# Two down tiles in block form, and four out-projection tiles summed onto the residual in PSUM

## The chip, the cores and the metric

The kernel runs on one core of a Trainium2 chip. The metric is the time of one execution on the device, in microseconds (us). A core has engines with queues of their own, each in order: TensorE (PE: matmuls, and PEld: the loads of their weights), VectorE (DVE), ScalarE (ACT), GpSimd (POOL) and SyncE (SP), which here only issues DMAs. Matmuls read SBUF and write PSUM, eight banks of 128 x 512 fp32; VectorE and ScalarE read and write both. Semaphores join the queues.

## The reference, cut to what matters

One layer of a hybrid encoder, for 512 tokens of a new stream and 64 of a running one, 576 columns in all. State-space heads and latent-attention heads give `y_ssd` and `o`; then:

```python
x = x + jnp.concatenate([y_ssd, o], axis=-1) @ p['w_out']
hf = rmsnorm(x, p['norm_ffn'])
x = x + (jax.nn.silu(hf @ p['w_gate']) * (hf @ p['w_up'])) @ p['w_down']
...
y_prompt = rmsnorm(xp, norm_final)
```

`D_MODEL` is 1024, so `x` has 8 tiles of 128 channels; `D_FF` is 2816, 22 tiles of 128. All data are fp32.

## The kernel before

All activations lie transposed: 128 channels on the partitions, 576 tokens along the row, worked on as two halves of 288 (`TH`). An fp32 product is made of three fast ones: each operand is split into a high part (a rounding cast, by ScalarE) and a low part (the rest, a subtraction by VectorE), and the matmuls are high x high, high x low, low x high. `split_weights` (lines 113, 114) does this for every 128 x 1024 piece of weights. So each weight costs ScalarE and VectorE time as well.

**Out-projection** (`out_tile`, line 728; `product_halves`, line 441). For each tile `t` of `x`, the sum over the four attention tiles, and for some tiles over the four state-space tiles too (those of the others were added earlier, the "F" steps of the order string), goes into a bank "hm", one for each half: 12 or 24 matmuls. Its `evac` then adds the bank to the residual `x2[t]` on VectorE (line 740):

```python
        def evac(ps, cols):
            dve.tensor_tensor(x2[t][:, cols], ps, x2[t][:, cols], ALU.add)
```

The tiles come in the order O0 O1 O2 O3 O5 O4 O6 O7, with the sums of squares (Q) and the operands of the next stage (`x_operands`, lines 797 to 805: scalings and casts by ScalarE, subtractions by VectorE) between them.

**Gate and up** (`gu_steps`; `block_product`, line 871). Gate and up of one 128-channel tile `f` and the two token halves form a 2 x 2 block product, made with seven products in place of eight (the Winograd form). Sums of weights (`block_weights`, lines 827 to 830) and of operands stand for the eighth. A tile is 7 x 4 x 3 = 168 matmuls, gathered in three banks x, y, z by steps m1, m6, m7, m2, m5, m4, m3. Between the steps ScalarE or VectorE takes results out of a bank to which the next step adds on. Each tile needs seven pieces of split weights in the ten buffers of `w2pool`, and four raw ones from the eight of `wpool`.

**Down**. The 22 tiles fall into parts 0-3, 4-7, 8-11, 12-15, 16-17 and 18-21. The first four parts use the same block form (`pair`, line 980; `down_steps`, lines 1004 to 1052; `down_blocks`): two pairs of tiles `f` against two tiles of `x` at a time, 7 x 2 x 3 matmuls, the first tile's results added to `x2[t]` by VectorE, those of the second gathered by ScalarE into SBUF and added by accumulating DMAs from GpSimd's queue (line 1022). They are placed among the products of the next part's first two tiles. Tiles 16 and 17 use the plain form (`down`, line 1081; matmuls of line 1077): for each of the eight `x` tiles a weight DMA, a split of 128 x 256, two groups of six matmuls and two additions by VectorE (line 1088). Tiles 18 to 21 make the end of the kernel together with the last norm; nothing of that changes.

**Order.** The program's own order is only a start. At the end `issue_in_order` reads the lists `ISSUE`, one for each engine, and ties each instruction to the one ahead of it. So each engine's order is written out, as numbers of instructions in program order. Buffers of the pools `tpool` (7 temporaries), `wpool` (8), `cpool` (5), `w2pool` (10) and the PSUM banks "hm" (2), "sc" (3), "pp" (3) rotate.

Of the kernel before, what the change touches and what calls it, by code (L numbers as in the profile page):

```python
# [37 lines left out]
BLOCKS = tuple(range(0, LAST - 1, 4))  # L38

# [16 lines left out]
def hybrid_layer_kernel(ctx: ExitStack, tc: tile.TileContext, a, o):  # L56
# [15 lines left out]
    cpool = ctx.enter_context(tc.tile_pool(name="cpool", bufs=5))  # L72
    a_, apool = open_pool("apool", bufs=4)
# [4 lines left out]
    def slot(pl, tag, name, **kw):  # L78
        return pl.tile([P, 2, T], F32, tag=tag, name=name, **kw)

    def tmp(name, w=T):
        return tpool.tile([P, UPW], F32, tag="t", name=name)[:, :w]
# [23 lines left out]
    def wslot(wp, name, dt=F32):  # L106
        return wp.tile([P, 1024], dt, tag="w", name=name)
# [330 lines left out]
    def bank(tag, name):  # L438
        return (psq if tag == "sc" else psh).tile([P, 512], F32, tag=tag, name=name, bufs={"sc": 3, "pp": 3, "hm": 2}[tag])

    def product_halves(terms, n, name, evac, hfs=(0, 1)):

        for hf in hfs:
            ps = bank("hm", f"{name}_{hf}")
            cols = slice(hf * n, (hf + 1) * n)
            for k, ((whi, wlo), (xhi, xlo)) in enumerate(terms):
                for i, (w, x) in enumerate(((whi, xhi), (whi, xlo), (wlo, xhi))):
                    pe.matmul(  # L448
                        ps[:, :n], w, x[:, cols], start=k == 0 and i == 0, stop=k == len(terms) - 1 and i == 2,
                    )  # L450
            evac(ps[:, :n], cols)
# [276 lines left out]
    def out_tile(hfs, t):  # L728
# [13 lines left out]
        product_halves(terms, TH, f"ps_o{hfs[-1]}_{t}", evac)  # L742
# [37 lines left out]
    w2pool = ctx.enter_context(tc.tile_pool(name="w2pool", bufs=10, reuse_waits="tile"))  # L780
    xop = ctx.enter_context(tc.tile_pool(name="xop", bufs=1, reuse_waits="tile"))
# [36 lines left out]
    def block_weights(src1, src2, name, blocks):  # L818
# [4 lines left out]
        shaped = lambda z: z if len(src1.shape) == 2 else z.rearrange("p (t c) -> p t c", t=2)  # L823
# [18 lines left out]
    held, blocks, fz2 = {}, [], []  # L842
# [74 lines left out]
    def finish(f, g, u):  # L917
        act.activation(g, g, AF.Silu)
        dve.tensor_tensor(u, u, g, ALU.mult)
# [53 lines left out]
    def paired(f, u):  # L973
# [3 lines left out]
        if k == 3 or f == BLOCKS[0] + 1:  # L977
# [26 lines left out]
    def down_steps(fs, w, h, p):  # L1004

        t = 4 * h + 2 * p
        qs = blocks[(fs[0] - BLOCKS[0]) // 2 :][:2]
        x, y, z = fbank("hm", f"ps_dx{fs[0]}_{t}"), fbank("sc", f"ps_dy{fs[0]}_{t}"), fbank("pp", f"ps_dz{fs[0]}_{t}")
        B, C = (tmp(f"d{i}{fs[0]}_{t}") for i in "bc")

        def sums(ps, i, onto=False):
            n, xi = PRODUCTS[i - 1]
            for k, q in enumerate(qs):
                whi, wlo = (z[:, 2 * p + k] for z in w[n])
                o = q[xi]
                for j, (l, r) in enumerate(((whi, o[:, 0]), (whi, o[:, 1]), (wlo, o[:, 0]))):
                    pe.matmul(  # L1017
                        ps, l, r, start=not onto and k == 0 and j == 0, stop=onto or (k == 1 and j == 2), skip_group_check=onto,
                    )

        def add_to(t, v):
            pool.dma_start(x2[t], v, accum_op=ALU.add)  # L1022
# [5 lines left out]
        def m6():  # L1028
            sums(x, 6, True)
            act.copy(B[:, :TH], x)  # L1030

        def m7():
            sums(z, 7)
            act.copy(C[:, TH:], z)
# [5 lines left out]
        def m5():  # L1040
            sums(x, 5, True)
            act.copy(B[:, TH:], x)  # L1042
            add_to(t + 1, B)

        def m4():
            sums(z, 4, True)
            act.copy(C[:, :TH], z)
# [8 lines left out]
    def down_blocks(fs, h, late):  # L1056
        w = down_weights(fs[0], h)
        if fs[0] == 0 and h == 0:
            Ri = tmp("Ri")
            dve.scalar_tensor_tensor(Ri, ss3, P / (D * EPS), R2, ALU.mult, ALU.mult)  # L1060
            for t in range(KT):
                dve.tensor_tensor(x2[t], x2[t], Ri, ALU.mult)
        for p in range(2):
            first, rest, middle = down_steps(fs, w, h, p)
# [4 lines left out]

    def down_terms(fs, t):  # L1070
        w = weights(a["w_down"][t][:, fs[0] * P : (fs[-1] + 1) * P], len(fs) * P, f"d{fs[0]}_{t}")
        return [(wk(w, k), prod[f]) for k, f in enumerate(fs)]
# [7 lines left out]

    def down(fs):

        for t in range(KT):
            terms = down_terms(fs, t)
            for hf, cols in enumerate(HC):
                ps = fbank(("hm", "sc", "pp")[(2 * t + hf) % 3], f"ps_d{fs[0]}_{t}")
                down_half(ps, terms, cols)
                dve.tensor_tensor(x2[t][:, cols], ps, x2[t][:, cols], ALU.add)
# [6 lines left out]
    for part in PARTS:  # L1095
        for f in part:
# [5 lines left out]
            if len(prev) == 4 and f in part[:2]:  # L1102
                late = down_blocks(prev, f - part[0], late)
                if f == part[1]:
                    if len(part) == 4:
                        late += (lambda f=f: pair(f),)
                    else:
                        late += tuple(lambda f=f: single(f, held.pop(f)) for f in part)
# [166 lines left out]

ISSUE = {
# [13 lines left out]
1190-1192 1227 1193-1198 1291-1297 1199-1201 1228 1202-1204 1286-1288 1207-1223 1318-1319 1224-1226 1298-1317  # L1290
1330-1333 1342-1343 1348-1355 1344-1347 1320-1329 1334-1341 1356-1392 1404-1405 1393-1401 1406 1402 1407-1409 1403
1410-1418 1428 1419-1427 1429-1430 1572 1431-1434 1440-1442 1435-1436 1443-1445 1437-1439 1446-1461 1464 1462
# [267 lines left out]
```

## Time and profile before

| | us |
|---|---|
| three runs shown | 645.3, 646.35, 1577.34 |
| median of them | 646.35 |
| profiled execution, its own time | 645.34 |
| its span, first to last instruction | 643.4 |
| PE busy | 631.6 |
| VectorE busy | 544.8 |
| ScalarE busy | 381.1 |

The 1577.34 is a single run far off the other two; the profiled execution agrees with the lower ones. In the profile's views, "idle before" is the time for which an engine stood still ahead of a group of instructions, and the arrow names what ended it. Busy times of pipelined matmuls overlap, so the number of matmuls that start in a stretch tells more than the share that is busy. Names of tiles are the program's with the numbers left out: `x<-ps_o,x` is an addition of a bank of the out-projection to the residual.

### The profile page before, as it was taken

How to read it: one execution, taken by the hardware profiler on the slowest of the kernel's cores; microseconds unless marked ns; L12 is line 12 of the kernel's file. 1: busy time of each engine (PE TensorE's matmuls, PEld its weight loads, DVE VectorE, ACT ScalarE, POOL GpSimd, SP SyncE). 2: the span in 40 equal slices, each digit the busy share in tenths (PEclk: the TensorE clock that was granted, in tenths of full speed). 3: DMA queues.
4: the chain of work that ended last, by engine and by line, in shares of the span. 5: the costliest groups of instructions: out<-in, count | busy, mean ns of one | idle time of the engine just before them, and what ended most of it. 6: DMA issues, size and time to landing. Idle time of an engine off the chain costs nothing.

```text
span 643.4 us, 11975 instructions
## 1 busy us (share of the span) xinstructions
PE 631.6 (98%) x4651; PEld 600.3 (93%) x4651; DVE 544.8 (85%) x974; ACT 381.1 (59%) x733; POOL 70.4 (11%) x111
## 2 busy tenths in 40 slices
PE   9999999999999999999999999999999999999995
PEld 9799999886797899899999999999999999999994
DVE  6999986899766699999998997989689886697664
ACT  7645425879766476765557465655664655354464
POOL 1422131101000000000012002100211020100022
PEclk9999999999999999999999999999999999999999
DMA  9521184314221232142286428552646243734004
GB/s 320 193 73 56 51 206 137 112 40 135 107 76 33 100 98 73 60 132 66 66 204 152 120 78 193 121 151 66 157 143 168 74 115 67 169 127 132 1 1 147
DMA packets 31656, 72.66 MB, mean 113 GB/s; under 512 B 3802, under 2 KB 11496, under 8 KB 31344
## 3 DMA queue, kind: packets, MB, share of 16 engines
q1 hardware_dynamic: 25456, 60.77, 29.4%
q0 software_dynamic: 5424, 10.57, 9.2%
q8 instruction: 36, 0.59, 0.4%
q10 hardware_dynamic: 720, 0.57, 0.3%
q14 instruction: 20, 0.16, 0.1%
HBM read 58.03 MB, written 3.30 MB: 95 GB/s over the span
## 4 chain that ended last, share of the span: by engine, by line
PE 83%; DVE 10%; ACT 3%; issue 2%; DMA 1%; POOL 0%; POOLq 0%; DVEq 0%; ACTq 0%
PE ps_x L871 20%; PE ps_z L871 10%; PE ps_dx L1017 8%; PE ps_in L129 8%; PE ps_o L448 6%; PE ps_y L871 5%; PE ps_dz L1017 4%; PE ps_z L448 4%; PE ps_first L129 2%; PE ps_d L1077 2%; PE ps_dy L1017 2%; PE ps_l L1077 2%; PE sc L662 2%; PE pv L709 1%; PE ptp L684 1%
## 5 line engine op out<-in xcount | busy, mean ns | idle before, releaser
L871 PE MATMUL ps_x<-xop,wh_gu_S 128*128 128x288 f32 x504 | 119.2, 297 | 0.0
L871 PEld LDWEIGHTS ps_x<-xop,wh_gu_S 128*128 128x128 f32 x504 | 85.2, 188 | 1.0 <-ACT ps_y L942 0.3
L871 PE MATMUL ps_x<-xop,wl_gu_S 128*128 128x288 f32 x252 | 73.5, 295 | 0.0
L113 ACT CAST wh_gu_S<-gu 128x1024 fp32r<-128x1024 f32 x44 | 46.4, 1054 | 23.0 <-PE ps_x L871 12.0
L114 DVE TENSOR_TENSOR wl_gu_S<-gu,wh_gu_S 128x1024 fp32r<-128x1024 f32 x44 | 53.4, 1219 | 4.8 <-ACT wh_gu_S L113 4.6
L871 PE MATMUL ps_z<-xop,gu_a 128*128 128x288 f32 x252 | 52.3, 295 | 0.0
L1022 POOL DMA_DIRECT2D x<-db x16 | 14.9, 991 | 304.7 <-ACT db L1042 162.1
L871 PEld LDWEIGHTS ps_x<-xop,wl_gu_S 128*128 128x128 f32 x252 | 47.2, 188 | 0.0
L129 PE MATMUL ps_in<-xs,wh_in 128*128 128x288 f32 x256 | 45.4, 298 | 0.0
L871 PE MATMUL ps_y<-xop,wh_gu_A 128*128 128x288 f32 x168 | 43.0, 297 | 0.3 <-ACT ps_y L942 0.3
L871 PE MATMUL ps_z<-xop,wh_gu_S 128*128 128x288 f32 x168 | 41.2, 296 | 0.5 <-DVE g L954 0.5
L871 PE MATMUL ps_x<-xop,wh_gu_A 128*128 128x288 f32 x168 | 41.2, 296 | 0.1
L871 PEld LDWEIGHTS ps_z<-xop,gu_a 128*128 128x128 f32 x252 | 40.1, 188 | 0.1
L129 PEld LDWEIGHTS ps_in<-xs,wh_in 128*128 128x128 f32 x256 | 37.7, 189 | 0.2
L114 DVE TENSOR_TENSOR wl_gu_A<-gu,wh_gu_A 128x1024 fp32r<-128x1024 f32 x22 | 26.8, 1219 | 4.2 <-ACT wh_gu_A L113 3.6
L871 PEld LDWEIGHTS ps_y<-xop,wh_gu_A 128*128 128x128 f32 x168 | 29.4, 188 | 0.7 <-ACT ps_y L942 0.6
L871 PEld LDWEIGHTS ps_z<-xop,wh_gu_S 128*128 128x128 f32 x168 | 28.8, 188 | 0.9 <-issue 0.7
L871 PEld LDWEIGHTS ps_x<-xop,wh_gu_A 128*128 128x128 f32 x168 | 28.9, 188 | 0.6 <-ACT wh_gu_A L113 0.3
L448 PE MATMUL ps_o<-cat_y,wh_out 128*128 128x288 f32 x128 | 28.5, 310 | 0.0
L448 PE MATMUL ps_o<-cat_o,wh_out 128*128 128x288 f32 x128 | 27.9, 298 | 0.0
L129 PE MATMUL ps_in<-xs,wl_in 128*128 128x288 f32 x128 | 27.5, 296 | 0.0
L113 ACT CAST wh_gu_A<-gu 128x1024 fp32r<-128x1024 f32 x22 | 23.1, 1051 | 6.5 <-PE ps_x L871 4.0
(557 smaller groups left out, 1973.2 us busy)
## 6 DMA issues: line engine op xcount, KB each, us to landing
gu<-in_w_gu SPq DMA_DIRECT2D x44, 512.0 KB, 4.1
db<-in_w_down SPq DMA_DIRECT2D x16, 512.0 KB, 3.8
x<-db POOLq DMA_DIRECT2D x16, 288.0 KB, 4.8
x<-dc POOLq DMA_DIRECT2D x16, 288.0 KB, 4.2
wr_in<-in_w_in SPq DMA_DIRECT2D x8, 512.0 KB, 6.1
wr_out<-in_w_out SPq DMA_DIRECT2D x8, 512.0 KB, 3.3
cumb<-cumD SPq DMA_DIRECT2D x5, 512.0 KB, 4.3
x<-in_xT SPq DMA_DIRECT2D x2, 1152.0 KB, 5.7
```

What stands on the lines that cost most here:

```text
L113: act.copy(hi, raw)
L114: dve.tensor_tensor(lo, raw, hi.bitcast(F32), ALU.subtract)
L129: pe.matmul(ps[:m, hf, :n], w, x[:, hf * n : (hf + 1) * n], start=start and k == 0 and i == 0, stop=stop and k == last and i == 2,)
L448: pe.matmul(ps[:, :n], w, x[:, cols], start=k == 0 and i == 0, stop=k == len(terms) - 1 and i == 2,)
L662: pe.matmul(s[:, :nk], qs[:, j, q0 : q0 + P], ks[:, j, :nk], start=True, stop=True)
L684: pe.transpose(pp[:, k : k + P], prs[p, i][:, j, b * P : b * P + P], ident)
L709: pe.matmul(pv[64 * j : 64 * j + 64, b * P :], V[b][:, h * HD : (h + 1) * HD], pts[p, b, j], start=b == 0, stop=True, skip_group_check=b > 0,)
L871: pe.matmul(ps, p, q, start=not onto and first and kp == kps[0] and j == 0, stop=onto or (last and kp == kps[-1] and j == 2), skip_group_c ...
L1017: pe.matmul(ps, l, r, start=not onto and k == 0 and j == 0, stop=onto or (k == 1 and j == 2), skip_group_check=onto,)
L1022: pool.dma_start(x2[t], v, accum_op=ALU.add)
L1077: pe.matmul(ps, w, x[:, cols], start=first and k == 0 and i == 0, stop=last and k == len(terms) - 1 and i == 2,)
```

## The change

1. **Out-projection, tiles 4 to 7** (`SEEDED`). ScalarE copies the residual half into the bank, all matmuls of the half add onto it, and ScalarE copies the sum back into `x2[t]`. VectorE's addition goes. The "F" steps keep the old form.
2. **Down tiles 16 and 17** in block form. One pair of `f` tiles, so that a product has 3 matmuls in place of 6; one set of block weights for all eight `x` tiles, used while tiles 18 and 19 run; the second `x` tile's results are added by VectorE from the bank, not by DMA.
3. **Fixed slots.** Each buffer of the four pools and each PSUM bank is taken by number from strings in `PLACES`, with as many buffers as before.
4. **New orders** for PE, VectorE, ScalarE and SP; GpSimd's is the same. PE has 12 instructions fewer (4392), VectorE 6 more (980), ScalarE 18 more (720), SP 6 fewer. PE's order is unchanged up to its 1278th instruction, VectorE's up to its 353rd, ScalarE's up to its 267th, SP's up to its 78th.

```diff
+SEEDED = (4, 5, 6, 7)
...
+    kept = {id(tpool): "t", id(wpool): "w", id(cpool): "c"}
+    counts = {}
+
+    def placed(pl, shape, dt, tag, name, bufs=None):
+
+        key = kept.get(id(pl), tag)
+        n = counts[key] = counts.get(key, -1) + 1
+        return pl.tile(shape, dt, tag=f"{key}{PLACES[key][n]}", name=name, bufs=1)
...
     def bank(tag, name):
-        return (psq if tag == "sc" else psh).tile([P, 512], F32, tag=tag, name=name, bufs={"sc": 3, "pp": 3, "hm": 2}[tag])
+        return placed(psq if tag == "sc" else psh, [P, 512], F32, tag, name)
...
-    def product_halves(terms, n, name, evac, hfs=(0, 1)):
+    def product_halves(terms, n, name, evac, hfs=(0, 1), base=None):
...
+            onto = base is not None
+            if onto:
+                act.copy(ps[:, :n], base[:, cols])
             for k, ((whi, wlo), (xhi, xlo)) in enumerate(terms):
                 for i, (w, x) in enumerate(((whi, xhi), (whi, xlo), (wlo, xhi))):
                     pe.matmul(
-                        ps[:, :n], w, x[:, cols], start=k == 0 and i == 0, stop=k == len(terms) - 1 and i == 2,
+                        ps[:, :n], w, x[:, cols], start=not onto and k == 0 and i == 0,
+                        stop=onto or (k == len(terms) - 1 and i == 2), skip_group_check=onto,
                     )
...
-        product_halves(terms, TH, f"ps_o{hfs[-1]}_{t}", evac)
+        if 1 in hfs and t in SEEDED:
+            product_halves(terms, TH, f"ps_o{hfs[-1]}_{t}", lambda ps, cols: act.copy(x2[t][:, cols], ps), base=x2[t])
+        else:
+            product_halves(terms, TH, f"ps_o{hfs[-1]}_{t}", evac)
...
     def down_weights(f, h):
-        src = a["w_down"][4 * h : 4 * h + 4, :, f * P : f * P + 512].rearrange("(t i) k c -> i k t c", i=2)
+        ts, n = (slice(4 * h, 4 * h + 4), 4) if h is not None else (slice(0, KT), 2)
+        src = a["w_down"][ts, :, f * P : (f + n) * P].rearrange("(t i) k c -> i k t c", i=2)
...
-        if f < BLOCKS[-1]:
+        if f < LAST:
             return paired(f, u)
-        if f < LAST:
-            held[f] = u
-            return
-        single(f, u)
-
-    def single(f, u):
         s = slot(cpool, "c", f"pr{f}")
...
-    def down_steps(fs, w, h, p):
+    def down_steps(fs, w, t, b, by_dma=True):
...
+        def out(v, cols, ps):
+            if by_dma:
+                act.copy(v[:, cols], ps)
+            else:
+                y = x2[t + 1][:, cols]
+                dve.tensor_tensor(y, ps, y, ALU.add)
+
         def add_to(t, v):
-            pool.dma_start(x2[t], v, accum_op=ALU.add)
+            if by_dma:
+                pool.dma_start(x2[t], v, accum_op=ALU.add)
...
+        if len(fs) == 4:
+            w = down_weights(fs[0], h)
+        elif h == 0:
+            wpair[0] = w = down_weights(fs[0], None)
+        else:
+            w = wpair[0]
...
-    def down(fs):
-
-        for t in range(KT):
-            terms = down_terms(fs, t)
-            for hf, cols in enumerate(HC):
-                ps = fbank(("hm", "sc", "pp")[(2 * t + hf) % 3], f"ps_d{fs[0]}_{t}")
-                down_half(ps, terms, cols)
-                dve.tensor_tensor(x2[t][:, cols], ps, x2[t][:, cols], ALU.add)
...
-            if len(prev) == 4 and f in part[:2]:
+            if prev and f in part[:2]:
                 late = down_blocks(prev, f - part[0], late)
...
-            elif prev and f == part[0]:
-                for step in late:
-                    step()
-                late = ()
-                down(prev)
...
+PLACES = {
...
+    "v": "".join("""
+0987654321908751432968751043964387926510437926843759120647358910647235069184735062913547809613524709618354709612354780
+912356470912834509761234508971234506971283406975123064897123056497128306497512306489797129730581267430589164732
```

The string "v" gives the slots of `w2pool` in program order. Near its end stand, seven each (one piece for A22, then high and low of A11/A12, of S1/S2 and of S3/S4): gate/up tile 18 `8306497`, the pair's down weights `5123064`, gate/up tile 19 `8979712`, tile 20 `9730581`, tile 21 `2674305`, and eight pieces for the end.

More of the change, by code (lines that the diff above doesn't have):

```diff
@@ L106, in wslot @@
     def wslot(wp, name, dt=F32):
+        if id(wp) in kept:
+            return placed(wp, [P, 1024], dt, "w", name)
         return wp.tile([P, 1024], dt, tag="w", name=name)
@@ L976, in paired @@
         k = (f - BLOCKS[0]) % 4
-        if k == 3 or f == BLOCKS[0] + 1:
+        if k == 3 or f == 1:
             pair(f)
@@ L1041, in m5 @@
             sums(x, 5, True)
-            act.copy(B[:, TH:], x)
+            out(B, HC[1], x)
             add_to(t + 1, B)
@@ L1046, in m4 @@
             sums(z, 4, True)
-            act.copy(C[:, :TH], z)
+            out(C, HC[0], z)
             add_to(t + 1, C)
```

360 lines of the change are left out of this document (198 added, 162 removed).

## The prediction

> **What bounds the kernel now.** I read the page's head first, then the busy times by stretches of 20 us, then what the weight loads of TensorE waited for.
>
> ```profile
> span 643.4 us, 11975 instructions
> ## 1 busy us (share of the span) xinstructions
> PE 631.6 (98%) x4651; PEld 600.3 (93%) x4651; DVE 544.8 (85%) x974; ACT 381.1 (59%) x733; POOL 70.4 (11%) x111
> ```
>
> TensorE (PE) is busy nearly all the time, so a change can win only matmuls that no longer exist, or the small holes that are left. The stretches show where the holes are (columns: stretch, length, then busy time and instruction count of PE, weight loads, VectorE, ScalarE, GpSimd, then the granted clock).
>
> ```profile
> 220.00:240.00 20.00, 20.00 (x150) 19.63 (x149) 19.53 (x33) 12.70 (x18) 0.00 (x0) 1.00 0.41 139
> 240.00:260.00 20.00, 19.50 (x141) 18.53 (x140) 20.00 (x41) 13.75 (x24) 0.00 (x0) 1.00 0.32 107
> 260.00:280.00 20.00, 19.86 (x140) 18.62 (x139) 20.00 (x35) 14.56 (x24) 0.00 (x0) 1.00 0.17 58
> 280.00:300.00 20.00, 19.66 (x148) 19.38 (x147) 19.98 (x34) 11.25 (x18) 0.00 (x0) 1.00 0.35 107
> 300.00:320.00 20.00, 19.79 (x149) 19.49 (x148) 19.97 (x34) 11.53 (x20) 0.00 (x0) 1.00 0.17 53
> ...
> 340.00:360.00 20.00, 20.00 (x153) 20.00 (x152) 18.12 (x30) 12.88 (x22) 3.44 (x4) 1.00 0.67 165
> ```
>
> In an undisturbed stretch 153 matmuls of 288 columns start in 20 us: one every 20/153 = 0.131 us. That pace, not the length of one matmul, prices a matmul that goes. From 220 to 320 us only 728 start where 5 x 153 = 765 would fit: 37 x 0.131 = 4.8 us of pace are lost there, at most (a few matmuls in it have other shapes). In the same 100 us VectorE (DVE) is busy 99.5 us. It holds the last out-projection tiles, the operands of gate and up, and the first weight splits.
>
> ```profile
> PEld ps_p L871 <- DVE xop L805: 0.8, 2, 0.4
> PEld ps_p L871 <- ACT xop L804: 0.7, 2, 0.4
> PEld ps_y L871 <- ACT ps_y L942: 0.6, 1, 0.6
> PEld ps_o L448 <- DVE x L740: 0.5, 2, 0.3
> PEld ps_dx L1017 <- ACT ps_dy L1026: 0.5, 1, 0.5
> PEld ps_x L871 <- ACT wh_gu_A L113: 0.3, 1, 0.3
> PEld ps_x L871 <- ACT ps_y L942: 0.3, 1, 0.3
> ```
>
> These are all waits of the weight loads between 220 and 320 us: 3.7 us. Two of them name VectorE; the ScalarE (ACT) ones are operands and weights whose inputs VectorE makes (line 804 casts what lines 798 to 801 subtract). So this stretch is bound by VectorE, the rest by TensorE's pace.
>
> **Out-projection tiles 4 to 7.** Eight additions on VectorE go (two halves, four tiles; line 740). In their place ScalarE copies the residual into the bank ahead of the matmuls and the sum out behind them.
>
> ```profile
> L740 DVE TENSOR_TENSOR x<-ps_o,x 128x288 f32<-128x288 f32 x30 | 13.5, 453 | 7.0 <-PE ps_o L448 6.8
> ```
>
> ```profile
> L1034 ACT COPY dc<-ps_dz 128x288 f32<-128x288 f32 x16 | 6.5, 403 | 6.3 <-PE ps_dz L1017 5.8 <-ACT db L1042 0.4
> ...
> L1026 ACT COPY ps_dy<-ps_dx 128x288 f32<-128x288 f32 x16 | 6.1, 387 | 5.3 <-PE ps_dx L1017 5.3
> ...
> L996 ACT CAST fz<-u 128x288 fp32r<-128x288 f32 x8 | 3.5, 433 | 0.8 <-DVE u L919 0.8
> ```
>
> VectorE loses 8 x 0.453 = 3.6 us in its full stretch. A copy out is 0.403 (line 1034, PSUM to SBUF). A copy from SBUF into PSUM has no row; it lies between 0.387 (PSUM to PSUM) and 0.433 (SBUF to SBUF, with a cast), and I take 0.39, since the destination is the same. ScalarE gains 8 x 0.79 = 6.3 us between about 230 and 260 us, where it is idle 40 - 12.70 - 13.75 = 13.6 us: it fits on average.
>
> The new wait is TensorE's: the first matmul into a bank now follows copy out and copy in, 0.79 us, where it followed an addition of 0.45. Two banks ("hm") alternate, and the order written out in the change puts 8 to 11 other matmuls between the last one of a bank and the first of its next owner, 1.05 to 1.44 us: covered by 0.26 us at the tightest, hand-over included. Behind one pair of copies ScalarE's order has a 128x576 cast and a 128x1024 cast ahead of the next pair; there I expect a hole of some tenths. If the cover were gone at all eight, it would cost 8 x 0.79 = 6.3 us.
>
> What the 3.6 us are worth lies between 0 (ScalarE becomes the late engine, its casts of line 804 stand between the copies) and 4.8 us (every lost slot of the stretch returns). Adding VectorE's durations along both written orders, I find the queue ahead of the sums of tiles 1 and 2 (lines 954, 966) shorter by 3 to 5 us, which leans to the upper part. The stretch is not bound by VectorE at every moment; I take **3.0 us**. What is late next is ScalarE.
>
> **Down tiles 16, 17.**
>
> ```profile
> L1077 PEld LDWEIGHTS ps_d<-pr,wh_d x64: 187/188/189, 552.8 to 571.1; 128*128 128x128 f32 x64
> L1077 PE MATMUL ps_d<-pr,wh_d x64: 288/295/313, 553.0 to 571.2; 128*128 128x288 f32 x64
> L1077 PEld LDWEIGHTS ps_d<-pr,wl_d x32: 187/188/193, 554.0 to 572.9; 128*128 128x128 f32 x32
> L1077 PE MATMUL ps_d<-pr,wl_d x32: 290/295/310, 554.2 to 573.0; 128*128 128x288 f32 x32
> ```
>
> (Columns: shortest, median and longest in ns, then first and last start.) These 96 matmuls go. The block form has 4 pairs of output tiles x 7 products x 3 = 84. Twelve fewer at 0.131 us are **1.6 us**; the stretches in which they lie run at full pace (below), so this comes off the end. The Trainium skill (Perfetto Trace Analysis, Identifying the Most-Contended Engine) says that pipelined matmuls make matmul time a bad measure and that the busy share of weight loads is the good one; by it the twelve would be an estimated 12 x 0.188 = 2.3 us, with the 188 ns above. The loads are 93% busy where matmuls start without a hole, so the pace decides here.
>
> The other engines pay:
>
> ```profile
> L114 DVE TENSOR_TENSOR wl_db_S<-db,wh_db_S 128x1024 fp32r<-128x1024 f32 x16 | 19.4, 1220 | 1.6 <-ACT wh_db_S L113 1.5
> ...
> L1088 DVE TENSOR_TENSOR x<-ps_d,x 128x288 f32<-128x288 f32 x16 | 7.0, 452 | 4.7 <-PE ps_d L1077 4.7
> ...
> L829 DVE TENSOR_TENSOR db<-db,db 128x512 f32<-128x512 f32 x8 | 5.5, 685 | 0.0
> ...
> L990 DVE TENSOR_TENSOR pv<-u 128x288 f32<-128x288 f32 x8 | 3.6, 451 | 0.0
> ...
> L114 DVE TENSOR_TENSOR wl_d<-wr_d,wh_d 128x256 fp32r<-128x256 f32 x8 | 3.3, 418 | 1.0 <-ACT wh_d L113 1.0
> ...
> L997 DVE TENSOR_TENSOR pb15x<-pv,pb15x 128x576 fp32r<-128x576 f32 x1 | 0.8, 755 | 0.0
> ```
>
> VectorE before: 16 x 0.452 + 8 x 0.418 + 2 x 0.755 = 12.1 us. After: 24 additions onto the residual (six for each pair, because the pair's second tile no longer goes by accumulating DMA) 10.8; weight sums and splits 5 x 0.685 + 3 x 1.220 = 7.1; operands 5 x 0.451 + 3 x 0.755 = 4.5: 22.4 us, so +10.3.
>
> ```profile
> L113 ACT CAST wh_db_S<-db 128x1024 fp32r<-128x1024 f32 x16 | 16.8, 1053 | 10.2 <-PE ps_x L871 5.1 <-PE ps_y L871 4.3 <-ACT wh_db_S L113 0.8
> ...
> L143 ACT ACTIVATE pr<-u 128x576 fp32r<-128x576 f32 x6 | 4.1, 691 | 1.9 <-DVE u L919 1.9
> ...
> L113 ACT CAST wh_d<-wr_d 128x256 fp32r<-128x256 f32 x8 | 3.3, 406 | 4.8 <-PE ps_d L1077 2.0 <-PE ps_x L871 1.9 <-PE ps_y L871 0.9
> ```
>
> ScalarE before: 8 x 0.406 + 2 x 0.691 = 4.6; after: 4 x 0.387 + 3 x 1.053 + about 0.6 for half a cast + 0.433 + 3 x 0.691 = 7.8: +3.2 us. Eight weight DMAs on SP become two of 512 KB; no wait for these weights is among those of TensorE, so I price that at nothing.
>
> ```profile
> 540.00:560.00 20.00, 20.00 (x152) 19.83 (x151) 11.79 (x21) 10.12 (x22) 3.14 (x4) 1.00 0.50 118
> 560.00:580.00 20.00, 20.00 (x152) 19.96 (x151) 18.75 (x35) 9.78 (x15) 0.33 (x1) 1.00 0.47 136
> 580.00:600.00 20.00, 20.00 (x150) 19.75 (x149) 15.15 (x23) 10.50 (x17) 0.00 (x0) 1.00 0.32 104
> 600.00:620.00 20.00, 20.00 (x143) 19.85 (x142) 12.14 (x20) 7.64 (x13) 2.73 (x3) 1.00 0.00 1
> ```
>
> VectorE is idle 80 - 57.8 = 22.2 us here, more than the 10.3 added, and TensorE has no hole to lose. Two waits are new. First, a product of only 3 matmuls (0.39 us) hands its bank to an addition of 0.45, four times in a row in bank x; that is hidden as long as the 336 matmuls of gate/up tiles 18 and 19 stand between. In the existing block parts the same hand-overs cost TensorE almost nothing in 16 pairs:
>
> ```profile
> PE ps_dx L1017 <- ACT ps_dy L1026: 0.2, 1, 0.2
> ```
>
> Second, weight slots. The pair's weights hold seven of the ten "v" slots across tiles 18 and 19 (5123064), so tile 19 (8979712) has to split its second weight pair into slots 9 and 7 of its own first pair, and its third into slots 1 and 2 that the down weights give up. The written order leaves 11 matmuls (1.44 us) for the cast of 1.05, and 21 (2.75 us) until the low part, after cast and subtraction 2.27: margins of 0.4 to 0.5 us. Bounds: nothing, or up to 7 us (below). I take **0.7 us** for all new waits together, near the measured 0.2.
>
> **Orders and slots.** The instruction orders are the same up to the 353rd VectorE instruction and the 1278th matmul instruction, both near 207 us, and for the last 109 of TensorE (from 620 us). So only 207 to 620 us can be better or worse. Fixed slots replace rotation with as many buffers; I price them at nothing, with some tenths either way.
>
> **Sum.** The profiled execution took 645.34 us (span 643.4 and 1.9 around it), 1.0 below the median shown and level with the fastest. 645.34 - 1.6 - 3.0 + 0.7 = **641.5 us**.
>
> **Rivals.** *ScalarE takes VectorE's place* between 230 and 310 us: casts and eight pairs of copies share one in-order queue, and only the twelve matmuls are won, less some tenths. For it speaks that line 804 already causes 0.7 us of waits; against it the 13.6 us of idle time. 645.34 - 1.6 + 0.5 = 644.2.
>
> *Slots come back late around tiles 19 to 21.* Five pairs of slots are refilled just in time (two for tile 19, three for tile 20). If each cast and each subtraction stands behind one more of its kind, as VectorE's added 10.3 us make possible, a high part is late by 1.05 - 0.4 and a low part by 1.22 - 0.5: 1.4 us a refill, 7.0 in all: 645.34 - 4.6 + 7.0 = 647.7, **slower than before**. It decides once the late arrivals sum to more than the 4.6 us won. Against it: VectorE's idle time there, and stretches that run at 150 to 152 matmuls with the same ten slots.
>
> *More is won:* all 4.8 us of the stretch return and the small holes after 420 us go too: 645.34 - 1.6 - 4.8 - 0.7 = 638.2.
>
> *The clock falls* in the new hand-overs, to half for the 96 matmuls of the seeded tiles: 96 x 0.131 = 12.6 us, 641.5 + 12.6 = 654.1. Against it: the clock reads 1.00 in every stretch above, those with seven waits too. The Trainium skill (TensorE: Matmul & The Clock Gate, A second HAM failure mode: psum-queue depth-cycling) describes such a fall where TensorE idles briefly and often between groups that cycle through banks; this trace, with 37 slots lost, shows none.
>
> **How the numbers follow.** Forecast 0.62 (639 to 643.7), ScalarE 0.16, late slots 0.13, more won 0.07, clock 0.02. The range 637.5 to 648 leaves out the clock, about half of the late slots and some of "more won", 0.1 to 0.15 in all. Faster by over 2% (below 633.4, against the median 646.35) would need more than all holes there are: 0.02; slower by over 2% (above 659.3): 0.02; within 2%, about what a measurement of this kernel can tell from no change: 0.96.
>
> **What would show it.** Right: no matmul into ps_d, and 84 more block sums of line 1017 than before; from 220 to 320 us more than 745 matmuls and VectorE below 98 us; line 740 22 times in place of 30; copies into ps_o near 0.39 us; TensorE at 150 or more between 540 and 600. Wrong: waits of the weight loads on ScalarE's ps_o copies or line 804 above 2 us; waits of ps_x on wh_gu_S or wl_gu_S after 560 us; a granted clock below 1.

## The result, and the profile after

The changed kernel takes 647.88 us in the median of seven runs, against 645.98 of before: a ratio of 1.0032, 95% interval 1.002 to 1.0044. So it is 1.9 us slower. The forecast was 641.5 us: 3.9 less by its terms (-1.6 - 3.0 + 0.7), and 4.5 less than this median. The change is below 2% and inside the range given, but it goes the other way. The profiled execution took 648.09 us, with this head of its page:

```profile
span 646.0 us, 11965 instructions
## 1 busy us (share of the span) xinstructions
PE 633.2 (98%) x4639; PEld 601.2 (93%) x4639; DVE 551.6 (85%) x980; ACT 389.6 (60%) x751; POOL 71.3 (11%) x111
```

TensorE issues the twelve instructions fewer that were counted, and still the span is 2.6 us longer. The twelve are worth 1.6 us at the pace, so TensorE must have lost 2.6 + 1.6 = 4.2 us of pace. The busy times by stretches show where (columns as in the prediction: length, then busy time and count of PE, weight loads, VectorE, ScalarE, GpSimd, then the granted clock, the DMA share and GB/s). First the stretch that was to gain:

```profile
220.00:240.00 20.00, 19.37 (x141) 18.63 (x140) 17.48 (x30) 11.09 (x18) 0.00 (x0) 1.00 0.44 147
240.00:260.00 20.00, 19.96 (x148) 19.42 (x147) 19.66 (x36) 18.84 (x38) 0.00 (x0) 1.00 0.23 75
260.00:280.00 20.00, 19.81 (x145) 19.26 (x144) 19.83 (x35) 15.09 (x27) 0.00 (x0) 1.00 0.28 95
280.00:300.00 20.00, 20.00 (x148) 19.55 (x147) 19.87 (x33) 12.03 (x20) 0.00 (x0) 1.00 0.35 103
300.00:320.00 20.00, 20.00 (x151) 19.83 (x150) 19.61 (x33) 10.69 (x20) 0.00 (x0) 1.00 0.18 57
```

From 240 to 320 us the rows count 592 matmuls, those of before 578: 14 x 0.131 = 1.8 us won. From 220 to 240 us there are nine fewer, 1.2 us lost. Over the whole stretch that is 733 against 728, where more than 745 had been asked for. Now two stretches for which next to nothing had been forecast, the gate and up tiles from 320 us on and the new place of the down tiles, one row for each (a matmul that runs across a row's edge is counted in both neighbours, so long rows count a little less than the sum of short ones). First the kernel before, then after the change:

```profile
320.00:420.00 100.00, 100.00 (x755) 99.88 (x754) 92.08 (x144) 59.74 (x106) 13.13 (x16) 1.00 0.57 144
540.00:600.00 60.00, 60.00 (x450) 59.55 (x449) 45.69 (x79) 30.40 (x54) 3.47 (x4) 1.00 0.43 119
```

```profile
320.00:420.00 100.00, 100.00 (x742) 98.86 (x742) 88.00 (x138) 59.38 (x103) 13.09 (x15) 1.00 0.55 138
540.00:600.00 60.00, 59.41 (x442) 58.67 (x441) 53.31 (x91) 32.62 (x53) 3.47 (x4) 1.00 0.41 117
```

In the first row nothing differs but orders and slots, and 13 matmuls fewer get done in the same 100 us: 13 x 0.131 = 1.7 us lost. The busy time reads 100.00 in both, and the view of waits lists nothing in this stretch for the weight loads of either kernel. The loss is made of pieces too small for that list. The count shows them, and so in part does the busy time of the weight loads, 98.86 us against 99.88. In the second row it is 8 matmuls, 1.1 us.

I set this out as pace lost: the time from each matmul's start to the next one's, less 0.1314 us for a full one of 288 columns and less the mean of before for other shapes, summed over all matmuls of a stretch. After less before is then: 0 to 200 us +0.4 (all of it in the first 20 us, where the traces of all thirteen kernels, with equal orders there, spread over 0.9 us, so this varies from run to run), 200 to 220 +0.6, 220 to 240 +1.1, 240 to 320 -2.0, 320 to 420 +1.6, 420 to 520 0.0, 520 to 620 +1.4, from 620 on +1.1: the 4.2, all told.

What the weight loads waited for from 220 to 320 us after the change:

```profile
PEld ps_o L465 <- DVE x L758: 1.1, 2, 0.7
PEld ps_o L465 <- ACT ps_o L462: 0.4, 2, 0.3
PEld ps_n L931 <- DVE nr_v L187: 0.4, 1, 0.4
PEld ps_x L894 <- DVE wl_gu_A L128: 0.2, 1, 0.2
```

2.1 us in place of 3.7, and ScalarE's copies into the banks (line 462) stand for only 0.4. From 520 to 620 us, where weight slots were expected to be tight:

```profile
PEld ps_z L894 <- DVE wl_gu_S L128: 0.8, 1, 0.8
```

At the end of the kernel, before and then after:

```profile
PEld ps_n L1193 <- ACT sq L1223: 0.3, 1, 0.3
PEld ps_r L1247 <- DVE Rp L179: 0.2, 1, 0.2
```

```profile
PEld ps_r L1257 <- DVE Rp L193: 0.7, 1, 0.7
PEld ps_n L1203 <- ACT sq L1233: 0.6, 1, 0.6
```

TensorE's order is the same there, VectorE's is too from 622 us on, and nothing of the work changed. ScalarE's order did. In its timeline after the change a scaling stands between two steps of the last norm, on the way to `Rp`:

```profile
635.35 0.28 ACT L186 ACTIVATE nr_y<-ps_n 128x128 f32<-128x128 f32 x1 [0.54 <-PE ps_n L1203]
635.53 0.55 ACT L1149 ACTIVATE x<-x,par 128x320 f32<-128x320 f32 x1
635.98 0.30 ACT L188 ACTIVATE nr_y<-nr_y 128x128 f32<-128x128 f32 x1
```

The second step starts 0.63 us behind the first; before the change it was 0.31. Of the 1.1 us lost at the end, 0.8 are in the two rows of waits.

The added instructions, from the groups after the change (the additions on the residual, ScalarE's copies in and out):

```profile
L758 DVE TENSOR_TENSOR x<-ps_o,x 128x288 f32<-128x288 f32 x22 | 9.9, 454 | 3.9 <-PE ps_o L465 3.8
...
L462 ACT COPY ps_o<-x 128x288 f32<-128x288 f32 x8 | 3.2, 404 | 1.4 <-DVE x L758 1.2
L761 ACT COPY x<-ps_o 128x288 f32<-128x288 f32 x8 | 3.2, 396 | 0.6 <-PE ps_o L465 0.3
```

### The profile page after: what moved, and what is told of

Same layout as the page of the kernel before. It is cut to its first block, busy times and chain, and to the rows that moved or that the text cites. A ratio compares the mean times of both kernels' runs of the same rounds, so it can differ in the third digit from the quotient of the medians.

```text
span 646.0 us, 11965 instructions
## 1 busy us (share of the span) xinstructions
PE 633.2 (98%) x4639; PEld 601.2 (93%) x4639; DVE 551.6 (85%) x980; ACT 389.6 (60%) x751; POOL 71.3 (11%) x111
## 4 chain that ended last, share of the span: by engine, by line
PE 81%; DVE 11%; DMA 2%; ACT 2%; issue 2%; POOL 0%; POOLq 0%; SPq 0%; DVEq 0%; ACTq 0%
PE ps_x L894 19%; PE ps_z L894 10%; PE ps_dx L1034 8%; PE ps_in L143 8%; PE ps_o L465 7%; PE ps_y L894 5%; PE ps_z L465 4%; PE ps_dz L1034 4%; PE ps_first L143 2%; PE ps_l L1104 2%; PE ps_dy L1034 2%; DMA gu<-in_w_gu 2%; PE sc L680 2%; PE pv L727 2%; PE ptp L702 1%
## 5 line engine op out<-in xcount | busy, mean ns | idle before, releaser
L894 PE MATMUL ps_x<-xop,wh_gu_S 128*128 128x288 f32 x504 | 126.4, 298 | 0.0
L894 PEld LDWEIGHTS ps_x<-xop,wh_gu_S 128*128 128x128 f32 x504 | 87.5, 188 | 1.3 <-DVE u L975 0.3
L894 PE MATMUL ps_z<-xop,gu_a 128*128 128x288 f32 x252 | 61.8, 298 | 0.0
L894 PE MATMUL ps_y<-xop,wh_gu_A 128*128 128x288 f32 x168 | 45.5, 298 | 0.0
L894 PEld LDWEIGHTS ps_z<-xop,gu_a 128*128 128x128 f32 x252 | 43.1, 188 | 0.6
L894 PE MATMUL ps_x<-xop,wh_gu_A 128*128 128x288 f32 x168 | 43.1, 297 | 0.0
L894 PE MATMUL ps_z<-xop,wh_gu_S 128*128 128x288 f32 x168 | 43.1, 296 | 0.0
```

The lines of the kernel that those rows point to most:

```text
L894: pe.matmul(ps, p, q, start=not onto and first and kp == kps[0] and j == 0, stop=onto or (last and kp == kps[-1] and j == 2), skip_group_c ...
```

## The experiments

After this result the theory was: the two edits of the work give what was forecast, and the new orders of the engines take it back, in many hand-overs that are a little late. The rivals: the copies by ScalarE give less than 3.0 us; the fixed slots cost; the clock or a contention takes it back.

**What a late hand-over costs.** From some 300 waits of both traces between 215 and 620 us I read this: a matmul that waits for VectorE or ScalarE starts 53 to 55 ns after the end of the instruction that releases it, at the earliest, and the matmul behind it 290 to 294 ns after that end. Without a wait, matmuls follow at 131 to 132 ns. So far that is a fit to two traces; runs 9 and 10 below test it. It means that a release has to come some 29 ns before the *preceding* matmul starts, 160 ns ahead of the waiting one, to be free.

**1. Some matmuls earlier, 320 to 540 us.** Of the changed kernel, at 31 late places in the middle, 40 matmuls that wait for nothing are issued a few places earlier, ahead of one that waits:

```diff
 ISSUE["PE"]
-2110-2112 2120 2113 2126 2139 2127-2128 2192 2121 2129-2130 2144-2145 2131 2122 2140 2132-2133 2146-2147 2134-2135
+2110-2112 2120 2113 2126 2139 2127-2128 2192 2121 2129-2130 2144-2145 2131 2122 2140 2132-2135 2146-2147 2141 2148
...
```

> The changed kernel with 40 matmuls of the stretch 320 to 540 us issued a few places earlier, each ahead of a weight load that the trace of the changed kernel shows waiting (31 places, 4.1 us of late arrivals); same instructions, same slots, same order on every other engine. Hand-over theory (a weight load whose operand or bank is released 0 to 150 ns too late costs TensorE that lateness; the new written orders put the hand-overs that tight): the waiting load stands one matmul later and finds its release in time, so most of the lateness goes, 1.5 to 3 us: 645 to 646.4. Slot theory (the fixed slots make weights late) and ScalarE theory (the copies around the seeded banks are what costs): neither weights nor copies change here, so within 0.5 us of the changed kernel's 647.9.

Measured 646.56 us, ratio 1.0015 (1.0003 to 1.0026), span 644.4: 1.1 us less than the change by the ratios, where 1.5 to 3 had been expected, and the two intervals overlap. Its row from 320 to 420 us stands next to that of before again:

```profile
320.00:420.00 100.00, 100.00 (x754) 99.73 (x752) 88.72 (x139) 60.03 (x105) 13.06 (x15) 1.00 0.55 140
```

So the loss in this row was the order of these matmuls: by the account of pace it is 0.2 us there, in place of 1.6. But not all of it reached the end: between 440 and 490 us TensorE now waits 0.9 us for a product of VectorE (line 983), where the changed kernel did not. Who catches up in one place can wait in the next.

**2 to 3. TensorE's order written anew, 221 to 620 us.** In the changed kernel and in the one before. The new order comes from replaying the trace's durations with the rule above: where the next matmul would come too early for its release, one that waits for nothing goes ahead, with the data dependences and the turn of each bank kept. All other engines' orders stay. In the kernels that ran, 1103 of TensorE's 4392 places differ, and 912 of 4404.

```diff
 ISSUE["PE"]   (after; the one before is treated alike)
-1351-1355 1347 1320-1326 1333-1335 1327-1329 1336-1341 1356-1363 1368-1370 1364-1367 1371-1378 1380-1388 1379
+1351-1355 1347 1320-1326 1333-1335 1327-1328 1336-1337 1329 1338-1340 1356 1341 1357-1366 1368-1374 1367 1375-1396
...
```

> The changed kernel with only the order of the matmuls between 221 and 620 us written anew (851 of 4392 places hold another matmul), so that hand-overs get room; same instructions, slots and orders of the other engines. Hand-over theory: late arrivals of 9 us in that stretch fall to some 3.5, so 5 to 6.5 us less than the changed kernel: 641.5 to 643, below the kernel before. Slot theory: a weight that comes late stays late whatever stands around it, at most 1 us less: about 647. ScalarE theory: only the part at 220 to 260 us can move, at most 1.5 us: 646.5.

> Control: the kernel before, with only the order of its matmuls between 221 and 620 us written anew in the same way (1130 of 4404 places). Hand-over theory: the kernel before has late arrivals of 8 us there, of which those at 240 to 280 us are VectorE's and can't be moved much, so 3.5 to 4.5 us less: 641.5 to 642.5, level with the changed kernel in its own new order. Slot and ScalarE theories say nothing of this kernel; if hand-overs cost nothing here, it stays at 646.

Measured 640.66 us (0.9927, 0.9911 to 0.9944) with the change, 641.18 (0.9934, 0.992 to 0.9949) without it, both a little under what was expected. The two long rows of the changed work in the new order:

```profile
320.00:420.00 100.00, 100.00 (x757) 100.00 (x756) 88.71 (x140) 59.04 (x103) 13.59 (x16) 1.00 0.57 145
540.00:600.00 60.00, 60.00 (x451) 59.65 (x450) 53.39 (x90) 32.93 (x50) 3.27 (x4) 1.00 0.36 100
```

Both counts, 757 and 451, are those of before or a little more. So 6.8 us of the changed kernel's time, by the ratios, stood in TensorE's order alone. The second run says something that I had not asked of the profile: the kernel *before* had 4.3 us in its order too. So 2.5 of the 6.8 us is what TensorE's order had worse after the change than before it. Given the same treatment, the two differ by 0.5 us, with intervals that overlap: less than the 3.9 that the change was to give. Part of the rest is in VectorE's and ScalarE's orders, which the change brought and these two runs keep: by the account of pace run 2 still loses 1.1 us from 200 to 240 us and 1.3 from 620 us on, against the kernel before. Run 8 changes these orders.

**4 to 6. The copies by ScalarE alone.** Taken out of the changed kernel; put into the one before in its own orders; and put into the one before with TensorE's order written anew.

```diff
 # 4, of the changed kernel
-SEEDED = (4, 5, 6, 7)
+SEEDED = ()
...
 # 5 and 6, of the kernel before; in 6 with ISSUE["PE"] written anew for it
+SEEDED = (4, 5, 6, 7)
...
-        product_halves(terms, TH, f"ps_o{hfs[-1]}_{t}", evac)
+        if 1 in hfs and t in SEEDED:
+            product_halves(terms, TH, f"ps_o{hfs[-1]}_{t}", lambda ps, cols: act.copy(x2[t][:, cols], ps), base=x2[t])
+        else:
+            product_halves(terms, TH, f"ps_o{hfs[-1]}_{t}", evac)
...
```

> The changed kernel without the seeded banks: the four out-projection tiles are added by VectorE as in the kernel before (eight additions back at the places of ScalarE's copies out, sixteen ScalarE copies gone); all else as in the changed kernel. Prediction's term (VectorE is relieved, 3.0 us): 2.5 to 3.5 us slower than the changed kernel, 650.5 to 651.4, with the loss between 240 and 280 us. ScalarE theory (the copies take VectorE's place and are part of what the change lost): 0.5 to 1.5 us faster than the changed kernel, 646.4 to 647.4. Slot theory and hand-over theory: nothing beyond the first term.

> The kernel before with the seeded banks alone (tiles 4 to 7 of the out-projection summed onto the residual in PSUM, copied in and out by ScalarE); matmuls in the order of the kernel before, ScalarE's copies put where the additions stood and where the banks come free. Hand-over theory: a bank now comes back 0.39 us later, behind copy out and copy in, and the old order leaves no room for it, so the late arrivals at 240 to 260 us rise from 1.6 to some 4 us and swallow what VectorE's relief gives: 1 to 3 us slower than before, 647 to 649. Prediction's term taken for itself (VectorE relieved of eight additions, 3.0 us, whatever the order): 642.6.

> The kernel before with the seeded banks alone, as in the run with the old order, and the order of the matmuls between 221 and 620 us written anew so that each hand-over finds its release in time. Hand-over theory: the seeds' gain appears once the order gives the copies room; late arrivals at 240 to 300 us fall from 3.9 us (kernel before in its new order) to some 2.5: 1 to 2 us less than the kernel before in its new order, 639 to 640.5. ScalarE theory (the copies take VectorE's place): no less than the kernel before in its new order, 641 or more.

Without the copies the changed kernel takes 650.49 us, 1.0078 (1.0063 to 1.0093): they are worth 0.0046 of 646, 3.0 us. By the account of pace 2.9 us of it lie between 240 and 320 us. The waits of its weight loads between 220 and 300 us name additions onto the residual (line 758) five times, 2.4 us, where the changed kernel had two, 1.1; its longest:

```profile
PEld ps_o L465 <- DVE x L758: 1.8, 4, 0.7
PEld ps_x L894 <- ACT g L911: 0.8, 1, 0.8
PEld ps_p L894 <- DVE x L758: 0.6, 1, 0.6
```

In the old orders the same copies make it slower: 648.69 us, 1.0044 (1.0029 to 1.0059). The view of waits, 220 to 320 us, says why:

```profile
PEld ps_o L452 <- ACT ps_o L449: 4.2, 7, 1.1
```

Seven of eight banks come late, because a bank now takes a copy out and a copy in (0.393 + 0.403 us, in ScalarE's queue behind whatever is ahead) where it took one addition. With TensorE's order written anew none of these seven waits is left, and it takes 640.27 us, 0.9914 (0.9897 to 0.993). That is 1.3 us under run 3 by the ratios, but the two intervals overlap, and TensorE's order differs from run 3's in 791 places, since each was written for its own kernel. So the worth of these copies is -2.8, some +1.3 (not clear of noise) or +3.0 us by the order that they stand in.

**7. The block form without the copies**, TensorE's order written anew, from the kernel of run 4:

```diff
 SEEDED = ()
 ISSUE["PE"]
-1351-1355 1347 1320-1326 1333-1335 1327-1329 1336-1341 1356-1363 1368-1370 1364-1367 1371-1378 1380-1388 1379
+1351-1355 1347 1320-1326 1333-1335 1327-1329 1336-1341 1356-1363 1368-1370 1364-1367 1371-1397 1404-1405 1398-1399
...
```

> The changed kernel without the seeded banks, the order of the matmuls between 221 and 620 us written anew for it: tiles 16, 17 in block form, fixed slots and the changed orders of the other engines are left. Hand-over theory: the stretches after 320 us lose next to nothing, and what is left at 240 to 280 us is VectorE's, 4.5 us: 5.5 to 7 us less than the changed kernel without seeds in its written order, 643.5 to 645. If slots or the block form cost by themselves, it stays above 647.

A miss: 646.71 us, 1.0016 (1.0007 to 1.0025), where 643.5 to 645 had been expected. From 240 to 280 us it stays as slow as run 4, 269 matmuls in both:

```profile
240.00:280.00 40.00, 37.55 (x269) 35.75 (x268) 39.44 (x75) 27.80 (x47) 0.00 (x0) 1.00 0.25 78
```

VectorE is busy 39.44 of 40 us there, and this order of TensorE did not help. But a full VectorE alone does not explain it: the kernel before has VectorE busy all the time and does ten matmuls more:

```profile
240.00:280.00 40.00, 39.36 (x279) 37.15 (x278) 40.00 (x75) 28.30 (x47) 0.00 (x0) 1.00 0.24 83
```

VectorE's own order is the likely rest; no run took that apart. And TensorE waits twice in a place where the changed kernel of run 2 does not, 440 to 480 us:

```profile
PEld ps_x L894 <- DVE g L983: 0.9, 1, 0.9
PEld ps_x L894 <- DVE wl_gu_A L128: 0.6, 1, 0.6
```

The first is the same wait that run 1 had met. Why VectorE's `g` is late here and not in run 2 stays open. So no run shows what the block form is worth by itself (1.6 us were taken). Beside the copies it shows no gain: run 2, which has it, is at 0.9927, and run 6, which does not, at 0.9914.

**8. VectorE's and ScalarE's orders too.** The kernel of run 2 with all three engines' orders written anew from 221 to 618 us, and from 204 to 219 us in the order that the kernel before has:

```diff
 ISSUE["PE"]   (DVE and ACT are treated alike)
-1190-1192 1227 1193-1198 1291-1297 1199-1201 1228 1202-1204 1286-1288 1215-1217 1207-1210 1218-1220 1211-1214
-1221-1222 1298 1223 1299 1224 1318 1225-1226 1319 1301-1302 1300 1303-1317 1330-1332 1342-1343 1348-1350 1344-1346
+1190-1192 1227 1193-1198 1291-1297 1199-1201 1228 1202-1204 1286-1288 1207-1223 1318-1319 1224-1226 1298-1317
+1330-1332 1342-1343 1348-1354 1344-1346 1355 1347 1320-1326 1333-1335 1327-1329 1336-1341 1356-1363 1368-1370
...
```

> The changed kernel with the orders of TensorE, VectorE and ScalarE written anew between 221 and 618 us, and the 204 to 219 us stretch in the relative order of the kernel before; slots and instructions as in the change. Hand-over theory: 0.5 to 1 us less at 200 to 240 us, 0.5 to 1 less in the tail after 620 us: 1 to 2.5 us less than the changed kernel with new matmul order alone, 638 to 639.7. If the tail and the 200 us stretch are not a matter of order, it is level with that one, 640.5.

Measured 639.54 us, 0.9902 (0.9887 to 0.9917), span 636.7: the fastest of all, 8.4 us under the changed kernel and 2.1 under run 3, both by the ratios. The work is that of the change, matmul for matmul. By the account of pace, 200 to 240 us now lose 0.3 us less than in the kernel before, and the end 0.4 more; the two waits at the end (ps_r and ps_n) read 0.2 us each, where run 2 still has 0.7 and 0.6. So this part of the loss was in the orders. But no run rewrote VectorE's and ScalarE's orders in the kernel before, so the 2.1 us are not what the two edits are worth, and run 8's interval overlaps with that of run 6, which has the copies alone. What is left to wait for between 220 and 320 us is ScalarE:

```profile
PEld ps_z L894 <- ACT nr_y L186: 1.2, 1, 1.2
PEld ps_z L894 <- ACT wh_gu_S L127: 0.6, 1, 0.6
```

**9 and 10. Hand-overs one and two places tighter.** In the kernel of run 8, at 35 places between 300 and 617 us, a matmul that waits is issued one place earlier, or two. Nothing else differs. By the rule, the first should cost about 0.08 us at each place, the second about 0.2; if a late wait cost a fixed toll, the two would cost the same.

```diff
 # 9 against 8, the first of 35 places in ISSUE["PE"]
-1972 1956 2026 1973 1976 1957-1961 1977 1974-1975 2027 1962-1965 2028 1978 1966-1969 2012 1979 2013 2029 1980-1981
+1972 1956 2026 1973 1976 1957-1961 1977 1974-1975 2027 1962-1965 2028 1978 1966-1968 2012 1969 1979 2013 2029
...
 # 10 against 9
-1972 1956 2026 1973 1976 1957-1961 1977 1974-1975 2027 1962-1965 2028 1978 1966-1968 2012 1969 1979 2013 2029
+1972 1956 2026 1973 1976 1957-1961 1977 1974-1975 2027 1962-1965 2028 1978 1966-1967 2012 1968-1969 1979 2013 2029
...
```

> The kernel of the run with all engines' orders rewritten, in which 35 matmuls between 300 and 600 us that wait for another engine change places with the matmul ahead of them; nothing else differs. In that run's trace each of the 35 finds its release in time by 2 to 107 ns, so a place of 132 ns earlier makes it 25 to 130 ns late, 2.7 us in sum. Hand-over theory, as a rule read from the traces (next start = the release + 291 ns, or the pace, whichever is later): 2.3 to 3 us slower than that run's 639.5, 642 to 642.5. If a wait that is a little late costs nothing (the order of one place cannot matter): 639.5.

> The same 35 matmuls two places earlier instead of one. Hand-over theory by the rule: each is later by another 132 ns, 2.7 + 35 x 0.132 = 7.3 us slower than the run with all engines' orders rewritten, 646 to 647.5. Rival (each late hand-over costs a fixed toll, whatever its lateness): as the run with one place, 642.

Measured 641.55 us (0.9938, 0.9921 to 0.9954) and 646.46 (1.001, 1.0001 to 1.002): 2.3 and 7.0 us over run 8 by the ratios, 2.8 and 7.8 by the spans. So two steps at 35 places undo most of the 8.4 us that run 8 had won over the changed kernel. One of the places, from the timeline of TensorE and ScalarE (start, duration, engine, line, what), in run 8:

```profile
324.93 0.29 PE L894 MATMUL ps_z<-xop,wl_gu_S 128*128 128x288 f32 x1
...
325.00 0.40 ACT L963 COPY u<-ps_x 128x288 f32<-128x288 f32 x1 [1.84 <-DVE db L851]
...
325.47 0.30 PE L894 MATMUL ps_z<-xop,wl_gu_S 128*128 128x288 f32 x1
...
325.60 0.30 PE L894 MATMUL ps_x<-xop,wh_gu_S 128*128 128x288 f32 x1
...
325.74 0.29 PE L1034 MATMUL ps_dx<-fz,wh_db_A 128*128 128x288 f32 x1
```

The copy frees bank x at 325.40, ahead of the matmul before the waiting one; that starts at 325.60, and the next 0.14 us later. No loss. In run 9:

```profile
325.70 0.29 PE L894 MATMUL ps_z<-xop,wl_gu_S 128*128 128x288 f32 x1
...
325.76 0.40 ACT L963 COPY u<-ps_x 128x288 f32<-128x288 f32 x1 [1.81 <-PE ps_x L894]
...
326.22 0.40 PE L894 MATMUL ps_x<-xop,wh_gu_S 128*128 128x288 f32 x1
...
326.46 0.30 PE L894 MATMUL ps_z<-xop,wl_gu_S 128*128 128x288 f32 x1
...
326.59 0.30 PE L1034 MATMUL ps_dx<-fz,wh_db_A 128*128 128x288 f32 x1
```

It frees the bank at 326.16, 0.06 before the waiting matmul starts, which is still in time. But the next comes only 0.24 us behind it, 0.30 after the release. In run 10:

```profile
326.56 0.29 PE L894 MATMUL ps_z<-xop,wl_gu_S 128*128 128x288 f32 x1
...
326.63 0.40 ACT L963 COPY u<-ps_x 128x288 f32<-128x288 f32 x1 [1.83 <-PE ps_x L894]
...
327.08 0.40 PE L894 MATMUL ps_x<-xop,wh_gu_S 128*128 128x288 f32 x1
...
327.32 0.29 PE L894 MATMUL ps_y<-xop,wh_gu_A 128*128 128x288 f32 x1
...
327.58 0.29 PE L1034 MATMUL ps_dx<-fz,wh_db_A 128*128 128x288 f32 x1
```

Again 0.05 and 0.29 us after the release (327.03), now with the lateness on top. From the first matmul shown to the last there are six steps, the same six matmuls in another order; they took 0.81, 0.89 and 1.02 us in the three runs; 35 x 0.08 = 2.8 and 35 x 0.21 = 7.4 us, near what the spans gained.

**11. Fixed slots alone.** The kernel before, with each buffer and bank in a numbered slot, the one that rotation had given it; orders unchanged.

```diff
+    def placed(pl, shape, dt, tag, name, bufs=None):
+        key = kept.get(id(pl), tag)
+        n = counts[key] = counts.get(key, -1) + 1
+        return pl.tile(shape, dt, tag=f"{key}{PLACES[key][n]}", name=name, bufs=1)
...
+PLACES = {
...
```

> The kernel before with fixed slots in place of the rotating pools, each tile in the very slot that it has in the kernel before; orders, instructions and everything else of the kernel before. Prediction (fixed slots at nothing) and hand-over theory: level with the kernel before within 0.5 us. Slot theory (fixing the slots costs by itself): 1.5 to 2 us slower.

Measured 646.15 us, 1.0009 (1.0 to 1.0019): 0.6 us, hardly told from nothing. Slots are not where the time went.

Its profiled execution was the slowest of its ten, 647.55 us, and shows something else. Two loads of gate and up weights around 220 us took 5.0 us to land (median), where they took 4.2 in the trace of the kernel before. VectorE's queue stood 0.5 us for them, and TensorE then waited for additions to the residual (between 218 and 242 us):

```profile
PEld ps_o L460 <- DVE x L752: 0.9, 2, 0.7
```

From 220 to 240 us 145 matmuls start there, where the kernel before has 150 with the same orders.

## Why the prediction was wrong

**The step that failed** is the paragraph "Orders and slots": "I price them at nothing, with some tenths either way", together with the sum's 0.7 us "for all new waits together". The slots cost 0.6 us at the middle of run 11's interval, which starts at nothing. The orders cost several microseconds, in four places: the end of attention and the first weight sums (200 to 240 us, +1.7), the gate and up tiles from 320 to 420 us (+1.6), the down tiles' new place (520 to 620 us, +1.4), the end (+1.1). For three of them the sum has no term, and in the fourth twice its 0.7 us were lost. Writing one engine's order anew in run 2 took off 6.8 us without touching the work, 2.5 more than in the kernel before. Run 1, runs 9 and 10, and the counts of matmuls show the mechanism from 300 us on: hand-overs from ScalarE and VectorE to TensorE that arrive less than 160 ns ahead. I had read a wait as hidden when it was not in the list of waits; in this kernel a hand-over can cost about 0.1 us there without a row.

**What stays open.** From 200 to 240 us a late DMA has a part (below), and run 11 shows a like loss in the orders of the kernel before, so how much of the 1.7 us is order alone is not shown. Nor is it shown what the two edits are worth when all engines' orders are written anew on both sides. With TensorE's order alone written anew it was 0.5 us (runs 2 and 3), not told from nothing.

**"Only 207 to 620 us can be better or worse"** was wrong by the end: TensorE's last 109 instructions keep their order, but ScalarE's do not, and 1.1 us was lost after 620 us.

**"Twelve fewer at 0.131 us are 1.6 us"**: the count is right, and the 1.6 closes the account above (4.2 - 1.6 = 2.6). That it comes off the end by itself was not shown (run 7). The reason given against the price by weight loads misread the page: 93% is their share of the whole span, and in the full stretch from 340 to 360 us they are busy 20.00 of 20 us. Loads of 0.188 us that start every 0.131 us overlap, so the pace is the price all the same.

**"Near the measured 0.2"**, in the 0.7 us: 0.2 is the row of the matmuls. The row of the weight loads for the same hand-over (ps_dx, line 1017) stands further up in the prediction and reads 0.5.

**"3.0 us" for the eight additions**: 3.0 in run 4, so the size was right; but it holds for the change's orders, which were made for the copies. The sentence "If the cover were gone at all eight" named a real risk: run 5, in the orders of the kernel before, shows 4.2 us of waits on seven of eight banks. In the changed kernel the cover was there, 0.4 us in two waits.

**Where VectorE stood** in the stretch: below 98 us, as forecast (96.5). But from 220 to 240 us its queue, in order, stood for a DMA. One of its waits between 215 and 242 us:

```profile
DVE gu L852 <- DMA gu<-in_w_gu: 1.2, 1, 1.2
```

This weight sum stands ahead of an addition to the residual, for which TensorE then waits (the 0.7 us of line 758 above). An engine that lost work gave none of it back while an instruction in its queue waited for something else.

**The rivals.** "ScalarE takes VectorE's place" was not so: 0.4 us on its copies. "Slots come back late" came true for one refill of five, 0.8 us (wl_gu_S, line 128), where 1.4 was priced for each: the forecast time of that rival, 647.7, is close to the median by chance; its mechanism carries only a small part. "The clock falls": the clock reads 1.00 in every stretch shown, those with the banks in turn too. The Trainium skill (TensorE: Matmul & The Clock Gate, A second HAM failure mode: psum-queue depth-cycling) describes a clock that falls when TensorE idles briefly between groups cycling through PSUM banks; no row here shows it. "More is won", at 638.2, was nearly within reach of the same work in other orders: 639.54 in run 8.

**The marks.** The additions of line 740 fell to 22 as said, and the copies took 0.404 and 0.396 us where 0.39 and 0.403 were taken. Two counts showed the failure: 733 matmuls from 220 to 320 us where more than 745 had been asked for, and 442 from 540 to 600 us where at least 150 in each 20 us had been asked for and 450 stood before. None of the signs set for "wrong" showed it: the one late refill stood before bank z, ahead of 560 us.

## What to carry to other kernels

When TensorE's pace is the bound and every engine's order is written out, an edit that saves work has no fixed worth: price it in the order that it will stand in, and treat a changed order as a term that can be the largest, not as nothing. To tell what an edit is worth, write the orders anew on both sides. Count the matmuls that start in equal stretches before and after, since a list of waits leaves out what is lost a tenth of a microsecond at a time. In this kernel a hand-over to TensorE was free when its release came before the matmul *ahead* of the waiting one started, so place one matmul more than the data needs.

## What the runs showed of the hardware that was not expected

A late semaphore costs TensorE more than its lateness. The waiting matmul starts 53 to 55 ns behind the release, but the one behind it not before 290 to 294 ns, where 131 is the pace; runs 9 and 10 put 2.8 and 7.8 us (by the spans) on 35 such places.

A ScalarE copy of 128 x 288 fp32 took 404 ns from SBUF to PSUM (line 462), 396 to 402 from PSUM to SBUF (lines 761 and 1040), and 387 from PSUM to PSUM (line 1051), all in the changed kernel. The Trainium skill (ScalarE: Activation LUTs, Step-by-step: what each stage is for) holds that ScalarE to PSUM is the faster way. The trace agrees where the source is the same, 387 against 396 to 402 out of PSUM; the copy out of SBUF is slower than both, so the source counts as well as the destination.
